# Two transformer blocks in one kernel: weight low parts move from GpSimd to VectorE, and a fold of squares to TensorE

## The chip, the cores and the metric

The kernel runs on one core of a Trainium2 chip. A core has five engines that run side by side, each with its own queue of instructions in program order: TensorE (PE in the profile, with its weight loads as PEld), VectorE (DVE), ScalarE (ACT), GpSimd (POOL) and SyncE (SP), which here only issues transfers. They wait for each other by semaphores. The metric is the device time of one execution in microseconds (us); lower is better.

## What is computed

The reference runs two transformer blocks over 256 tokens (the first with 16 extra ones in front) and 1024 features, all in float32:

```python
# block 1
xn = rms_norm(h, gain0)
proj = xn @ w_in                       # q, k, v of two attentions, forget gate, two gates
o_a, o_b = forgetting_attention(...), stick_breaking_attention(...)
mixed = (sigmoid(g_a) * (o_a @ w_o_fox) + sigmoid(g_b) * (o_b @ w_o_sb)) @ w_out
h = h + rms_norm(mixed, gain1)
u = causal_depthwise_conv(rms_norm(h, gain2) @ w_up, conv_w, conv_b)   # 2 x 2816 features
h = h + rms_norm((gelu(u_gate) * u_val) @ w_down, gain3)
# block 2
proj = rms_norm(h, g_mix) @ w_in_2     # differential attention, retention, two gates
...
return rms_norm(x, g_final)
```

Block 2 goes on with attention, retention, a squared-ReLU feed-forward, a gated embedding and the last norm.

## The kernel before

**Split products.** Every large product is made of three products of a reduced float32 form (`float32r`): each operand is split into a high part (ScalarE's copy into `float32r`) and a low part (the operand less its high part). `mm3`, `feat_tile` and `token_tile` issue high x high (L320, or L333 with tokens as rows), weight low x feature high (L321, L334) and weight high x feature low (L323, L336).

**Weights.** `Weights` streams the weights as slabs of 256 or 512 columns. Each slab is two units (half slabs of 512 KB, one tile of 128 x 1024). SyncE loads a unit into one of `RAW` = 5 raw buffers; `split_unit` has ScalarE make its high part (`whi`, L87); `finish` makes the low parts still owed (`wlo`, L96) and issues the next loads. VectorE makes them, but GpSimd does where `finish` is called with `True`, and each fourth one while `ws.share` is 4. At most two slabs are split ahead. `start` splits one unit (two where the lead is short), and `next` hands a slab to TensorE.

**Order of the work.** The program order is written out by hand. After each tile of products (one bank of PSUM, four banks in turn) `period` runs: it starts a unit, advances the evacuations of earlier tiles by one stage (`side.evac`), lets one side task go on (`side.tick`) and finishes the low part. So on VectorE each tile's evacuation and the unit's low part come one after the other. `linear` runs a list of tiles; with `wave=3` it begins with three tiles chunk by chunk of the 1024 features, so that chunks can be used as they are made.

**The places that the change touches**, in order of time:

- `ev_mix` (L829) evacuates the second attention's output projection: product with the gate, sum, ScalarE's high part of the mixed features, and in its second stage their low part (`xl`, L835), on GpSimd for the first six of eight chunks.
- The next projection (`w_out`) collects sums of squares: VectorE adds the squares up (L400, `acc`), and TensorE sums them over the features with a matrix of ones (L392). After its last tile `period` is called without finishing, and `residual` (L876) follows: statistics (`rstd_narrow`), `ws.finish(True)` (L882), the broadcast of the result (L415), and then `make(k)`, which produces chunk k of the next input: VectorE's product with the gain, the addition to the residual `R` (GpSimd from the second chunk on, L897), ScalarE's high part and square, VectorE's low part. The up projection's first wave of three tiles consumes the chunks as they come.
- The up projection with a causal convolution (22 slabs, 44 tiles; `ev_conv`, L961): per tile VectorE scales the bank (`ur`, L302) and adds two shifted products (`cv`, L308, a pair of instructions), ScalarE adds bias and third tap (L969), and, by kind of tile, ScalarE's gelu or VectorE's product of both halves with its split follows. `ws.share = 4` holds here (L983).
- The down projection (L1012 on) walks four column groups, each over slabs of 6, 8 and 8 feature chunks, for two token tiles. Before it ScalarE loads another function table (L1011). Ahead of the last slab stands `ws.start(2)`, `ws.finish(True)`. Then `down_rstd` and `down_scale` give the normed rows, which TensorE turns (`turn_raw`, L1044).
- Block 2's first products (L1080 on): for token tile t and chunk k, `normed` updates the residual, `high` and `low` split it, and TensorE uses the chunk at once in two banks. For the statistics `squares` has ScalarE square four chunks at a time; after the second four GpSimd folds eight blocks into two (L1065), and `mix_sums` sums these two over the features (L1070); `mix_rstd` makes the reciprocal root from it. For t = 1 two units are started (k = 2 and 4) and finished on GpSimd (k = 3 and 5).

Of the kernel before, what the change touches and what calls it, by code (L numbers as in the profile page):

```python
# [20 lines left out]
KD = D // P  # L21
# [28 lines left out]
class Weights:  # L50
    """Streams weight slabs: DMA, then an exact split into two float32r parts."""

    def __init__(self, nc, raw, hi, lo, plan):
        self.nc, self.rawp, self.hip, self.lop = nc, raw, hi, lo
        self.plan = plan
        self.raw, self.parts = {}, {}
        self.loaded = 0
        self.units = 0
        self.todo = []
        self.at = 0  # L60
        self.share = self.lows = 0

# [27 lines left out]

    def finish(self, idle=False):
        for lo, w, hi in self.todo:
            self.lows += 1
            idle = idle or self.share and self.lows % self.share == 0
            eng = self.nc.gpsimd if idle else self.nc.vector
            eng.tensor_tensor(lo, w, f32(hi), ALU.subtract)  # L96
        self.todo = []
        self.load(self.units + RAW)
# [22 lines left out]
class Side:  # L121
    """Advances evacuations and queued side tasks by one stage per call."""

# [46 lines left out]
def two_blocks_kernel(  # L170
# [64 lines left out]

# [1 line left out]
    tab = cp.tile([P, 256], F32, name="tab")  # L237
# [52 lines left out]

# [1 line left out]
    def bank(pool, tag):  # L292
# [81 lines left out]
    class Sums:  # L374
        """Sums of squares over features, with tokens on the partitions."""

# [47 lines left out]

    def period(gen=None, finish=True):
        ws.start()
        side.evac()
        if gen is not None:
            side.evacs.append((0, gen))
        side.tick()  # L430
        if finish:
            ws.finish()
# [70 lines left out]

# [1 line left out]
    R = cp.tile([P, KD, NQ], F32, name="R")  # L505
# [101 lines left out]

# [1 line left out]
    u4 = unit("u4", shape=(P, KD, L1))  # L609
# [209 lines left out]

# [1 line left out]
    def ev_fox(ps, j):  # L821
# [7 lines left out]
    def ev_mix(ps, j):  # L829
        t = tp_tile("t", NQ)  # L830
        mul(t, ps[:, :NQ], gb[:, j, :])
        add(t, t, ga[:, j, :])
        A.activation(xh[:, j, 0:NQ], t, AF.Copy)
        yield
        (G if j < 6 else V).tensor_tensor(xl[:, j, 0:NQ], t, f32(xh[:, j, 0:NQ]), ALU.subtract)  # L835

# [39 lines left out]
    def residual(sums, after, toks, off, n, gout, gnext, fill):  # L876
        """The next linear's input from a normed residual: a maker of one chunk at a time."""
        side.evac()
        fill(0)
        side.flush()  # L880
        y = sums.rstd()
        ws.finish(True)  # L882
        fill(1)
        pb = at()
        bcast(pb, y, toks)
        fill(2)
        hi = unit("xh", F32R, (P, KD, L1))
        lo = unit("xl", F32R, (P, KD, L1))
        sqs = {}

        def res(k):
            return R[:, k, off:off + n]

        def normed(k, eng):
            t = tp_tile("t", n)
            stt(t, raw[:, k, 0:n], g1(gout + k), pb[:, :n])
            eng.tensor_tensor(res(k), res(k), t, ALU.add)  # L897

        def high(k):
            A.activation(hi[:, k, 0:n], res(k), AF.Identity, scale=g1(gnext + k))  # L900
            sqs[k] = after.tile(n)
            A.activation(sqs[k], res(k), AF.Square)

        def make(k):
            if k == 0:
                normed(0, V)
                normed(1, G)
                high(0)
            if k + 2 < KD:
                normed(k + 2, G)  # L910
            if k + 1 < KD:
                high(k + 1)
            stt(lo[:, k, 0:n], res(k), g1(gnext + k), f32(hi[:, k, 0:n]), ALU.mult, ALU.subtract)
            if k in (4, 6):
                ws.start(1)
            if k in (5, 7):
                ws.finish()
            if k in (0, 1, 5, 6):
                fill(3)
            return sqs[k]  # L920
        return chunks(hi, lo), make
# [11 lines left out]
    def ple_filler(W, stages):  # L933
        """Spreads the embedding's products over a residual's waits: one bank at a time."""
        held = []

        def fill(stage):
            if stage == 3:
                dst, src = held.pop(0)
                A.activation(dst, src, AF.Copy)  # L940
                return
            for t, c in stages[stage]:
                ps = at() if len(held) < 3 else mm()
                ts, cs = slice(t * P, (t + 1) * P), slice(c, c + 512)
                for k in range(2):
                    mm3(ps, ph[:, k, ts], pl[:, k, ts], W[0][:, k, cs], W[1][:, k, cs], k == 0, k == 1)
                held.append((ple[:, t, cs], ps))
        return fill

    box = {}  # L950

# [1 line left out]
    s1 = Sums(TOKQ, acc=True, mixed=True)  # L953
# [7 lines left out]
    def ev_conv(ps, j):  # L961
# [11 lines left out]
        if not val:  # L973
# [8 lines left out]

    ws.share = 4  # L983
    linear(feat_tiles(KF1, X2, 0, NQ), KD, ev_conv, wave=3, make=make, sums=s1,
           after=next_rstd(s1, NQ, [(rb2, 1.0)], box))
    ws.share = 0
    rawt = unit("u7", shape=(P, 2, D))
# [24 lines left out]
    for c in range(4):  # L1012
        pss = [mm(), mm()]
        for k0, nk in DOWN:
            W = ws.next()
            last = k0 + nk == KF1
            if c == 3 and last:
                ws.start(2)
                ws.finish(True)
            for t in range(2):  # L1020
# [9 lines left out]

# [1 line left out]
    hi = unit("xh", F32R, (P, KD, L1))  # L1032
# [27 lines left out]
    def squares(t, i):  # L1060
        A.activation(sqs[:, t, 4 * i:4 * i + 4, :],
                     R[:, 4 * i:4 * i + 4, 2 + t * P:2 + (t + 1) * P], AF.Square)
        if i:
            for n in (4, 2):
                G.tensor_tensor(sqs[:, t, 0:n, :], sqs[:, t, 0:n, :], sqs[:, t, n:2 * n, :], ALU.add)  # L1065

    def mix_sums(t):
        ps = turned[t] = at()
        for i in range(2):
            T.matmul(ps[:, 0:1], sqs[:, t, i, :], ones[:, 0:1], start=i == 0, stop=i == 1)  # L1070

# [12 lines left out]
    for t in range(2):  # L1084
# [3 lines left out]
        for k in range(KD):  # L1088
# [7 lines left out]
            if t == 0:  # L1096
                if k == 1:
                    y = down_rstd(1)
                if k == 2:
                    down_scale(1, y)  # L1100
            elif k in (2, 4):
                ws.start(1)
            elif k in (3, 5):
                ws.finish(True)
            for part in range(2):
# [216 lines left out]

# [1 line left out]
    def ev_brd(ps, j):  # L1324
# [44 lines left out]

# [1 line left out]
    gh = [unit(f"u{i}", F32R) for i in (0, 1, 2, 4)]  # L1371
# [37 lines left out]

# [1 line left out]
    gfin = unit("u0", shape=(P, D))  # L1411
# [90 lines left out]
```

## Time and profile before

| | us |
|---|---|
| median of 3 runs (range) | 951.78 (950.01 to 952.24) |
| profiled execution, first to last instruction (its span; the page gives no other time for it) | 950.2 |
| TensorE busy | 923.9 (97%) |
| VectorE busy | 648.3 (68%) |
| ScalarE busy | 523.5 (55%) |
| GpSimd busy | 91.5 (10%), 75 instructions |
| TensorE clock granted, mean | 0.988 |

The span is the time between the first and last instruction of one profiled execution; the runs are timed from outside and are 1.6 us longer in the median. A busy engine is one with an instruction under way; the products of TensorE are pipelined, so that their durations overlap (0.28 us long, 0.12 us apart). Averages over the whole span mix stages with different limits.

### The profile page before, as it was taken

Reading aid. Unit: us, or ns where it says so; the run is one execution under the profiler, and the core shown is the slowest. Engines: PE = TensorE matmul, PEld = TensorE weight load, DVE = VectorE, ACT = ScalarE, POOL = GpSimd, SP = SyncE. Lnnn points to the kernel's source line nnn. Section 1 sums busy time; section 2 is a strip of 40 time slices with the busy share of each in tenths; the row PEclk is TensorE's granted clock in tenths of the full one; section 3 lists DMA queues with packets and bytes.
Section 4 is the critical chain, followed back from the end, with each engine's and each line's share of the span. In section 5 each row is a group of like instructions: output and inputs, shape, how many; then the busy total and the mean of one; then the engine's idle time right before and its main releaser. Section 6 shows DMA issues by size and latency. Waiting matters only on the chain.

```text
span 950.2 us, 18312 instructions
## 1 busy us (share of the span) xinstructions
PE 923.9 (97%) x7457; PEld 894.6 (94%) x7457; DVE 648.3 (68%) x1150; ACT 523.5 (55%) x948; POOL 91.5 (10%) x75
## 2 busy tenths in 40 slices
PE   7999999999999999899899999999999999999996
PEld 5999988999899999899899999999999999999996
DVE  4667664577699999734767774577787666655546
ACT  5534565466576666545656665445555565544435
POOL 4022100022332222001300000000000000000000
PEclk7999999999999999899999999999999999999998
DMA  8554434456255565565265556455475566565531
GB/s 263 156 156 122 121 90 111 133 180 210 89 156 178 178 179 178 167 208 179 90 202 157 152 170 192 139 165 170 136 225 173 177 200 185 177 209 179 187 130 45
DMA packets 149715, 154.73 MB, mean 163 GB/s; under 512 B 5260, under 2 KB 145808, under 8 KB 149632
## 3 DMA queue, kind: packets, MB, share of 16 engines
q1 hardware_dynamic: 147904, 149.56, 52.4%
q0 software_dynamic: 1376, 3.36, 1.1%
q8 instruction: 58, 0.95, 0.4%
q10 hardware_dynamic: 352, 0.66, 0.2%
q14 instruction: 25, 0.20, 0.1%
HBM read 152.50 MB, written 1.05 MB: 162 GB/s over the span
## 4 chain that ended last, share of the span: by engine, by line
PE 79%; DVE 15%; issue 2%; ACT 2%; DMA 1%; POOL 0%; SPq 0%; DVEq 0%; ACTq 0%
PE mm L320 20%; PE mm L323 19%; PE mm L321 19%; DVE cv L308 5%; DVE wlo L96 4%; PE mm L336 4%; PE mm L334 4%; PE mm L333 4%; DVE ur L302 2%; PE at L671 1%; DVE cv L302 1%; DMA raw<-in_w_in_dram 1%; PE at L735 1%; PE at L1156 1%; DVE u L981 1%
## 5 line engine op out<-in xcount | busy, mean ns | idle before, releaser
L87 ACT ACTIVATE whi<-raw 128x1024 fp32r<-128x1024 f32 (+1 forms) x284 | 292.3, 1047 | 186.5 <-PE mm L323 90.9
L96 DVE TENSOR_TENSOR wlo<-raw,whi 128x1024 fp32r<-128x1024 f32 (+1 forms) x267 | 325.0, 1225 | 100.1 <-ACT whi L87 99.8
L323 PE MATMUL mm<-xl,whi 128*128 128x258 f32 (+2 forms) x1256 | 351.4, 283 | 1.3 <-DVE xl L308 1.3
L320 PE MATMUL mm<-xh,whi 128*128 128x258 f32 (+3 forms) x1192 | 342.8, 288 | 3.4 <-ACT xh L542 3.4
L321 PE MATMUL mm<-xh,wlo 128*128 128x258 f32 (+3 forms) x1192 | 337.5, 284 | 0.3 <-DVE wlo L96 0.3
L323 PEld LDWEIGHTS mm<-xl,whi 128*128 128x128 f32 x1256 | 235.8, 189 | 2.0 <-DVE xl L308 1.7
L320 PEld LDWEIGHTS mm<-xh,whi 128*128 128x128 f32 (+1 forms) x1192 | 225.1, 189 | 7.0 <-ACT xh L542 3.4
L321 PEld LDWEIGHTS mm<-xh,wlo 128*128 128x128 f32 (+1 forms) x1192 | 225.2, 189 | 1.6 <-DVE wlo L96 1.2
L320 PE MATMUL mm<-u,whi 128*128 128x256 f32 (+1 forms) x704 | 198.4, 282 | 0.0
L321 PE MATMUL mm<-u,wlo 128*128 128x256 f32 (+1 forms) x704 | 197.1, 280 | 0.0
L323 PE MATMUL mm<-u,whi 128*128 128x256 f32 (+1 forms) x576 | 162.6, 282 | 0.0
L321 PEld LDWEIGHTS mm<-u,wlo 128*128 128x128 f32 x704 | 133.1, 189 | 0.0
L320 PEld LDWEIGHTS mm<-u,whi 128*128 128x128 f32 x704 | 132.5, 188 | 0.0
L323 PEld LDWEIGHTS mm<-u,whi 128*128 128x128 f32 x576 | 108.4, 188 | 0.0
L333 PE MATMUL mm<-whi,u 128*128 128x256 f32 x240 | 68.7, 286 | 2.4 <-ACT whi L87 2.4
L334 PE MATMUL mm<-wlo,u 128*128 128x256 f32 x240 | 68.9, 287 | 1.5 <-DVE wlo L96 0.9
L336 PE MATMUL mm<-whi,u 128*128 128x256 f32 x240 | 68.6, 286 | 0.0
L308 DVE SCALAR_TENSOR_TENSOR cv<-ur,gc,cv 128x256 f32<-128x256 f32 x88 | 66.3, 756 | 1.6
L96 POOL TENSOR_TENSOR wlo<-raw,whi 128x1024 fp32r<-128x1024 f32 x17 | 40.8, 2405 | 176.1 <-ACT whi L87 94.2
L302 DVE TENSOR_TENSOR u<-mm,rb 128x256 f32<-128x256 f32 (+2 forms) x68 | 28.9, 425 | 40.1 <-PE mm L323 40.1
L333 PEld LDWEIGHTS mm<-whi,u 128*128 128x128 f32 x240 | 46.4, 193 | 2.6 <-ACT whi L87 2.6
L334 PEld LDWEIGHTS mm<-wlo,u 128*128 128x128 f32 x240 | 46.6, 194 | 1.9 <-DVE wlo L96 1.1
(343 smaller groups left out, 1088.4 us busy)
## 6 DMA issues: line engine op xcount, KB each, us to landing
raw<-in_w_in_dram SPq DMA_DIRECT2D x102, 512.0 KB, 3.8
raw<-in_w_ff_dram SPq DMA_DIRECT2D x64, 512.0 KB, 3.9
raw<-in_w_up_dram SPq DMA_DIRECT2D x44, 512.0 KB, 3.6
raw<-in_w_out_dram SPq DMA_DIRECT2D x16, 512.0 KB, 4.4
raw<-in_w_down_dram SPq DMA_DIRECT2D x16, 512.0 KB, 4.8
raw<-in_w_branch_diff_dram SPq DMA_DIRECT2D x8, 512.0 KB, 3.5
raw<-in_w_branch_ret_dram SPq DMA_DIRECT2D x8, 512.0 KB, 3.4
raw<-in_w_ple_gate_dram SPq DMA_DIRECT2D x8, 512.0 KB, 3.8
```

The source lines that it names most:

```text
L87: self.nc.scalar.activation(hi[:, a:b], w, AF.Copy)
L96: eng.tensor_tensor(lo, w, f32(hi), ALU.subtract)
L302: V.tensor_tensor(o, a, b, ALU.mult)
L308: V.scalar_tensor_tensor(out=o, in0=a, scalar=s, in1=b, op0=op0, op1=op1)
L320: T.matmul(ps, sh, mh, start=first, stop=False)
L321: T.matmul(ps, sl, mh, start=False, stop=False)
L323: T.matmul(ps, sh, ml, start=False, stop=last)
L333: T.matmul(ps[:, 0:256], hi, W[0][:, k, :], start=first, stop=False)
L334: T.matmul(ps[:, 0:256], hi, W[1][:, k, :], start=False, stop=False)
L336: T.matmul(ps[:, 0:256], lo, W[0][:, k, :], start=False, stop=last)
L671: T.matmul(S[:, 0:258], k[:, 0:128], q, start=False, stop=False, skip_group_check=True)
L735: T.matmul(o, l, i, start=False, stop=True, skip_group_check=True)
```

## The change

Low parts of weights are always VectorE's: `finish` has no choice of engine any more, and `share` is gone. All eight low parts of the mixed features are VectorE's. In the last tile before the residual no unit is started; one is started behind the statistics and finished after chunk 1. Between the blocks the two units are started at chunks 2 and 5 and finished at 4 and 7. GpSimd folds no squares; TensorE sums all eight blocks. GpSimd keeps its additions to the residual and half of the sums `acc` there.

```diff
-    def finish(self, idle=False):
+    def finish(self):
         for lo, w, hi in self.todo:
-            self.lows += 1
-            idle = idle or self.share and self.lows % self.share == 0
-            eng = self.nc.gpsimd if idle else self.nc.vector
-            eng.tensor_tensor(lo, w, f32(hi), ALU.subtract)
+            self.nc.vector.tensor_tensor(lo, w, f32(hi), ALU.subtract)
...
-    def period(gen=None, finish=True):
-        ws.start()
+    def period(gen=None, split=True):
+        if split:
+            ws.start()
         side.evac()
...
-        if finish:
+        if split:
             ws.finish()
...
-        (G if j < 6 else V).tensor_tensor(xl[:, j, 0:NQ], t, f32(xh[:, j, 0:NQ]), ALU.subtract)
+        V.tensor_tensor(xl[:, j, 0:NQ], t, f32(xh[:, j, 0:NQ]), ALU.subtract)
...
         y = sums.rstd()
-        ws.finish(True)
+        ws.start(1)
         fill(1)
...
-            if k in (5, 7):
+            if k in (1, 5, 7):
                 ws.finish()
...
-    ws.share = 4
     linear(feat_tiles(KF1, X2, 0, NQ), KD, ev_conv, wave=3, make=make, sums=s1,
            after=next_rstd(s1, NQ, [(rb2, 1.0)], box))
-    ws.share = 0
...
                 ws.start(2)
-                ws.finish(True)
+                ws.finish()
...
-        if i:
-            for n in (4, 2):
-                G.tensor_tensor(sqs[:, t, 0:n, :], sqs[:, t, 0:n, :], sqs[:, t, n:2 * n, :], ALU.add)
...
-        for i in range(2):
-            T.matmul(ps[:, 0:1], sqs[:, t, i, :], ones[:, 0:1], start=i == 0, stop=i == 1)
+        for i in range(KD):
+            T.matmul(ps[:, 0:1], sqs[:, t, i, :], ones[:, 0:1], start=i == 0, stop=i == KD - 1)
...
-            elif k in (2, 4):
+            elif k in (2, 5):
                 ws.start(1)
-            elif k in (3, 5):
-                ws.finish(True)
+            elif k in (4, 7):
+                ws.finish()
```

## Rows read from the trace of the kernel before

**Rows 1.** The page, the chain that ended last: share of the span by engine

```profile
PE 79%; DVE 15%; issue 2%; ACT 2%; DMA 1%; POOL 0%; SPq 0%; DVEq 0%; ACTq 0%
```

**Rows 2.** Stretches: length, busy us (instructions) of PE, PEld, DVE, ACT, POOL; clock; DMA

```profile
203.00:216.00 13.00, 13.00 (x110) 12.93 (x109) 11.82 (x22) 6.51 (x12) 7.90 (x8) 1.00 0.55 172
...
311.08:322.85 11.77, 11.77 (x100) 11.77 (x99) 11.63 (x20) 7.69 (x12) 2.40 (x2) 1.00 0.61 181
346.36:358.13 11.77, 11.76 (x98) 11.55 (x97) 11.63 (x20) 7.70 (x12) 2.40 (x2) 1.00 0.61 180
376.00:400.00 24.00, 20.12 (x142) 19.46 (x141) 18.48 (x29) 14.00 (x22) 2.37 (x1) 0.86 0.55 172
392.00:394.00 2.00, 2.00 (x11) 2.00 (x11) 2.00 (x3) 1.62 (x2) 0.00 (x0) 0.50 0.58 176
```

**Rows 3.** Timeline of VectorE: start us, us, engine, line, operation, out<-in, count

```profile
214.80 0.41 DVE L835 TENSOR_TENSOR xl<-t,xh 128x258 fp32r<-128x258 f32 x1
...
233.85 3.42 DVE L96 TENSOR_TENSOR wlo<-raw,whi 128x1024 fp32r<-128x1024 f32 x1
...
309.80 1.22 DVE L96 TENSOR_TENSOR wlo<-raw,whi 128x1024 fp32r<-128x1024 f32 x1
...
311.27 3.01 DVE L308 SCALAR_TENSOR_TENSOR cv<-ur,gc,cv 128x256 f32<-128x256 f32 x2
...
314.87 1.00 DVE L308 SCALAR_TENSOR_TENSOR cv<-ur,gc,cv 128x256 f32<-128x256 f32 x2
...
384.52 0.42 DVE L302 TENSOR_TENSOR ur<-mm,rb 128x258 f32<-128x258 f32 x1
...
445.69 1.59 DVE L308 SCALAR_TENSOR_TENSOR nt<-ny,nh 128x1 f32<-128x1 f32 x1 [0.41 <-ACT ny L362]
...
458.93 1.76 DVE L308 SCALAR_TENSOR_TENSOR nt<-ny,nh 128x1 f32<-128x1 f32 x1
460.73 2.27 DVE L308 SCALAR_TENSOR_TENSOR nr<-nt,ny 128x1 f32<-128x1 f32 x1
```

**Rows 4.** Timeline of GpSimd: in brackets the idle time before and what ended it

```profile
233.76 2.42 POOL L96 TENSOR_TENSOR wlo<-raw,whi 128x1024 fp32r<-128x1024 f32 x1 [17.58 <-ACT whi L87]
...
263.90 4.95 POOL L96 TENSOR_TENSOR wlo<-raw,whi 128x1024 fp32r<-128x1024 f32 x2 [7.69 <-ACT whi L87]
...
311.08 2.40 POOL L96 TENSOR_TENSOR wlo<-raw,whi 128x1024 fp32r<-128x1024 f32 x1 [9.36 <-DVE wlo L96]
...
381.08 2.37 POOL L96 TENSOR_TENSOR wlo<-raw,whi 128x1024 fp32r<-128x1024 f32 x1 [8.83 <-ACT whi L87]
442.52 4.75 POOL L96 TENSOR_TENSOR wlo<-raw,whi 128x1024 fp32r<-128x1024 f32 x2 [59.06 <-ACT whi L87]
...
458.28 4.70 POOL L96 TENSOR_TENSOR wlo<-raw,whi 128x1024 fp32r<-128x1024 f32 x2 [1.06 <-ACT whi L87]
```

**Rows 5.** Timeline of TensorE: in brackets its wait and what ended it

```profile
238.29 0.59 PE L392 MATMUL at<-ones,acc 128*86 128x1 f32 x6 [1.60 <-DVE acc L400]
...
376.83 0.28 PE L333 MATMUL mm<-whi,u 128*128 128x256 f32 x1
...
383.51 0.38 PE L334 MATMUL mm<-wlo,u 128*128 128x256 f32 x1 [0.62 <-POOL wlo L96]
...
390.31 0.39 PE L333 MATMUL mm<-whi,u 128*128 128x256 f32 x1 [2.39 <-ACT whi L87]
...
448.01 1.06 PE L1044 MATMUL at<-tab,u 128*128 128x128 f32 x8 [1.04 <-DVE u L1008]
...
457.83 0.50 PE L1070 MATMUL at<-ones,u 128*128 128x1 f32 x4
458.19 0.36 PE L333 MATMUL mm<-whi,xh 128*128 128x256 f32 x1
...
463.75 0.51 PE L336 MATMUL mm<-whi,xl 128*128 128x256 f32 x2 [2.71 <-DVE xl L308]
```

**Rows 6.** Timeline of ScalarE: the table load before the down projection

```profile
387.91 1.28 ACT L1011 ACT_TABLE_LOAD   x1
```

More of the change, by code (lines that the diff above doesn't have):

```diff
@@ L60, in __init__ @@
         self.at = 0
-        self.share = self.lows = 0
     def load(self, upto):
```

## The prediction

> **What bounds the kernel now.** I read the page's chain first, then the table of stretches, then each engine's own timeline around the seventeen places where GpSimd makes a low part. The chain that ends last is 79% TensorE and 15% VectorE [rows 1]: TensorE sets the pace, and the question is where VectorE makes it wait. In the table of stretches [rows 2] the reader is to see three things. First, TensorE's own rate: 110 products are listed in the 13.00 us from 203, two of them straddling an edge, so 13.00/108 = 0.120 us each. Second, in the feed-forward's up projection VectorE is busy 11.63 us of 11.77, that is, always. One turn of that loop is two slabs: four tiles of 24 products, 96 in all. At 311.08 TensorE still gets 98 products into 11.77 us (100 listed less two straddlers), its free rate; at 346.36 it gets 96, VectorE's rate. So TensorE is barely the faster (96 x 0.120 = 11.52 us against 11.77) and runs on its four banks of slack until they are used up. Third, the bill comes at the end: from 376 to 400 only 142 products are listed in 24.00 us, and at 392 the granted clock is 0.50, the 1.2 GHz level.
>
> The timelines say why VectorE is slow. In each turn it runs one pair of `cv` instructions in 3.01 us where the next pair of the same shape takes 1.00 [rows 3]; the slow pair, at 311.27, starts just behind GpSimd's low part (311.08 for 2.40 us) and gets going when that ends [rows 4]. It is so for all twelve low parts of this projection, from 263.90 to 381.08. The same shows outside it. GpSimd's low part at 233.76 lies over a VectorE low part of 3.42 us where 1.22 is usual. The two at 442.52 lie over a step of 1.59 us on one column. The two at 458.28 lie over two such steps of 1.76 and 2.27 us [rows 3, 4]. TensorE waits behind these: 1.60 us before L392, 1.04 before L1044, 2.71 before L336 [rows 5].
>
> **The up projection, twelve low parts.** On VectorE one costs 1.22 us [rows 3]; the duration overstates it a little, since neighbours overlap at their ends. What goes is the stretch, 3.01 - 1.00 = 2.01 us. VectorE's turn becomes 11.77 - 2.01 + 1.22 = 10.98 us, below TensorE's 11.52: VectorE stops being the bound and catches up. In all it is relieved of 12 x 0.79 = 9.5 us. It now starts the last tile's evacuation at 384.52 [rows 3], 7.7 us after TensorE went on to the down projection at 376.83 [rows 5]; so the lateness goes, and the last tiles wait for TensorE instead.
>
> What hangs on that lateness: ScalarE's table load at 387.91 [rows 6] stands behind the last `cv` work, 3.4 us after that evacuation, and the third down slab's high and low parts behind the load; TensorE ran out of work there and waited 2.39 us, after 0.62 for a GpSimd low part at 383.51 [rows 5]. It can run the first two down slabs without the table: 14 chunks x 2 token tiles x 3 = 84 products, 10.1 us. In before the third slab's high part served TensorE at 390.31, 5.8 us after the last evacuation began, and its low part is 1.22 us more. If TensorE enters the projection near 376 it needs them at 386, so the last evacuation must begin by 379; I put it at 376 to 377. The stall goes, with 2 to 3 us to spare, and with it what followed, a stretch at the lower clock. Its worth: 24.00 us less 140 products at 0.120 is 7.2 us; and the three last turns lost two products each, 6 x 0.12 = 0.7. Sum 7.9 us. Bounds: VectorE saves less per low part and a stall of some 3 us is left (5 us gained), or the last turns also run freer (8.5).
>
> The Perfetto Trace Analysis page of the Trainium skill (Optimizing Scalar/DVE Operations) says that with a saturated VectorE moving some work to ScalarE, or even GpSimd, may pay, though it adds that those two share a read port of SBUF. By the first half this change is wrong and would cost the whole 12 x 1.22 = 14.6 us; by the row, where the move slows VectorE by more than it takes away, it gives 9.5 us of VectorE's time back. The SBUF page (Who interferes with whom) has the sharper form, that a VectorE instruction with two SBUF inputs is blocked for the whole of a GpSimd one; 3.01 us over 2.40 agrees with it.
>
> **The mixed features, six low parts (L835).** TensorE does not stop here now; its windows are full. VectorE takes six more instructions of 0.41 us [rows 3]. Five of them come before the product that frees the bank of the third tile of the next projection's first wave, 5 x 0.41 = 2.0 us; VectorE has 13.00 - 11.82 = 1.2 us idle there [rows 2], and the waves leave no bank over. So TensorE is later by something between nothing and 2.0; I take 0.7. GpSimd's two transfers behind these low parts are issued no later, and are needed several us on.
>
> **The first residual.** The high part of one half slab moves behind the statistics, where ScalarE waits, and costs nothing; its low part goes from GpSimd to VectorE after chunk 1. The 3.42 us instruction becomes 1.22, the sum of squares behind it is done before TensorE asks, and the 1.60 us wait goes. Against it stands 1.22 us in the chain that makes the eight chunks, with the next chunk's low part and GpSimd's next addition queued behind it; between nothing (if TensorE's lag covers it) and 1.22 shows up. I take 0.8. Net 0.8 gained. The raw buffer comes free some ten us later, so one slab load starts later; four more are in hand, so I cost that at nothing; without this cover it would be a few us of DMA.
>
> **Between the blocks.** The two low parts at 442 go on an idle VectorE (nothing runs there until the statistics at 445), so the step of 1.59 shrinks and the wait of 1.04 goes. The two at 458 move to other chunks (started at 2 and 5, finished at 4 and 7), behind the reciprocal root instead of over it; 1.76 + 2.27 us of stretched steps go, and with them the wait of 2.71. The folds leave GpSimd, and TensorE sums eight blocks of squares in place of two. It has four instructions for two now, and the next product starts 0.36 us later [rows 5]: 0.09 each, so six sums more are 12 x 0.09 = 1.08 us, twice 2.2 us. Ends: nothing if they fall into waits, 3.0 by the 0.50 us of four instructions. I take 2.2, since after the waits are gone TensorE has work there all the time. Net 1.04 + 2.71 - 2.2 = 1.6 gained.
>
> **Sum.** -7.9 + 0.7 - 0.8 - 1.6 = -9.6 us. The profiled span is 950.2 us, the runs' median 951.78, so 1.6 us lie around it: 940.6 in a profile, 942.2 in the runs.
>
> **Rivals.**
> - *The stretch is not GpSimd's doing* (the pair waits for ScalarE's `cv`, say), so VectorE pays for the twelve low parts and gets nothing back: 14.6 us in the up projection, and 2.2 of sums: 951.8 + 16.8 = 968.6, slower. It decides from the point where less than 1.22 of the 2.01 us comes back. For it: VectorE is full there. Against: every stretched instruction lies over a GpSimd one, and so do the one-column steps, which have no such partner. Chance 0.03. (It is where the first half of the Trainium skill's sentence on a saturated VectorE, above, would lead.)
> - *The stall at the table load stays*, because the load itself and the chain behind it are too long: then 0.7 + 0.6 + 0.8 - 0.7 + 1.6 = 3.0 gained, 948.8, within the noise. Against: the 2 to 3 us to spare. Chance 0.05.
> - *VectorE's queue takes the place of GpSimd's* in the small stages: mix +1.4, residual 0, between the blocks only 1.04 against 2.2: 7.9 - 1.4 - 1.2 = 5.3 gained, 946.5. For it: low parts now stand in front of chunks that TensorE asks for every 0.7 to 1.1 us. Chance 0.12.
> - *The small costs are hidden*: mix 0, residual 1.6 gained, sums free: 13.3 gained, 938.5. Chance 0.10.
>
> **Numbers.** The forecast, 942.2 (its own range 939.5 to 944.5), has 0.70. The range 938 to 947 takes in the bounds of the unknown costs and the two near rivals, and leaves out some 0.15. A measurement of this kernel tells about 0.3%, 2.9 us. The forecast, the third and the fourth case are faster by more (0.92); the second is about that bound (0.05); the first is slower (0.03).
>
> **What the new profile would show.** The pairs of `cv` at 1.00 us throughout; VectorE with idle time in the up projection; 98 products in each 11.77 us of it to the end; the last evacuation within 1 us of TensorE's last tile; no gap and no lower clock after the table load; no wait before L392, and none of over 1 us before L336; L1070 with some 1.1 us more each time. I am wrong if VectorE's instructions are stretched without GpSimd, if the down projection still halts, or if new waits appear behind VectorE's low parts in the residual.

## The result and the profile after

The changed kernel takes 940.25 us (median of 4 runs, 939.66 to 942.12) beside 951.92 us of the kernel before (4 runs, 950.01 to 952.24): ratio 0.9883, 95% interval 0.9872 to 0.9895. It is 1.2% faster. The forecast was 942.2 us with a range of 938 to 947. The profiled execution has a span of 940.3 us (its own time is 942.12, 1.8 more), 9.9 less than before; the forecast for the span was 940.6.

First the page of the changed kernel: the chain that ended last, by engine, and then the busy time of each engine (us, share, instructions).

```profile
PE 94%; DVE 3%; ACT 1%; DMA 1%; issue 0%; POOL 0%; SPq 0%; DVEq 0%; ACTq 0%
...
PE 924.5 (98%) x7481; PEld 895.4 (95%) x7481; DVE 637.3 (68%) x1173; ACT 524.7 (56%) x948; POOL 40.4 (4%) x48
```

VectorE was 15% of the chain [rows 1] and is 3%. Of the 27 instructions that GpSimd gave up (75 became 48) VectorE took 23, the low parts, and yet its busy time fell, from 648.3 us to 637.3: an instruction that is held in the middle of its work counts as busy. The group of `cv` instructions shows it. It is the same 88 instructions of the same shape in both kernels, at 756 ns each before (66.3 us in all) and at 480 ns after:

```profile
L304 DVE SCALAR_TENSOR_TENSOR cv<-ur,gc,cv 128x256 f32<-128x256 f32 x88 | 42.0, 480 | 1.6
```

The 24.3 us that went are 2.02 for each of the twelve low parts that GpSimd made there.

The table of stretches of the changed kernel (columns as in [rows 2]) has the same places:

```profile
203.00:216.00 13.00, 12.41 (x104) 12.22 (x103) 12.73 (x27) 5.52 (x11) 0.00 (x0) 1.00 0.52 166
...
346.00:358.00 12.00, 12.00 (x103) 12.00 (x102) 11.43 (x22) 7.98 (x13) 0.00 (x0) 1.00 0.58 180
...
376.00:400.00 24.00, 24.00 (x205) 24.00 (x204) 14.47 (x20) 13.10 (x20) 0.00 (x0) 1.00 0.62 189
392.00:394.00 2.00, 2.00 (x20) 2.00 (x19) 1.20 (x1) 2.00 (x5) 0.00 (x0) 1.00 0.62 212
```

From 346 to 358, 101 products (103 listed less two straddlers) run in 12.00 us, 0.119 each: TensorE's own rate, and VectorE has idle time. In the first line, where VectorE took over the mixed features' low parts, it goes the other way: 104 products are listed where 110 were, and VectorE is idle for 0.27 us where it was for 1.18. The biggest gain is in the third line: 205 products from 376 to 400 where 142 were, at the full clock where 0.86 was the mean and 0.50 the lowest.

To split the 9.9 us, I marked the same products in both TensorE timelines and compared the stretches between them:

| stretch between marks of TensorE | before, us | after, us | difference |
|---|---|---|---|
| start to the first product of `w_out` | 212.91 | 212.71 | -0.2 |
| to the sums of squares held for the residual | 25.38 | 24.35 | -1.0 |
| to the first product of the up projection | 7.68 | 7.37 | -0.3 |
| up projection, first wave of three tiles | 10.52 | 11.95 | +1.4 |
| rest of the up projection | 120.34 | 119.51 | -0.8 |
| down projection, to the turn behind it | 71.18 | 62.46 | -8.7 |
| turn and first products of block 2, to the second broadcast | 24.40 | 24.31 | -0.1 |
| the rest | | | -0.2 |

The marks themselves, in TensorE's timeline of the changed kernel, with the waits that are left around them:

```profile
214.22 0.35 PE L316 MATMUL mm<-xh,whi 128*128 128x258 f32 x1 [0.59 <-DVE t L298]
...
237.06 0.40 PE L388 MATMUL at<-ones,acc 128*86 128x1 f32 x4
...
249.19 0.63 PE L319 MATMUL mm<-xl,whi 128*128 128x258 f32 x3 [0.34 <-DVE xl L304]
...
252.36 0.63 PE L319 MATMUL mm<-xl,whi 128*128 128x258 f32 x3 [0.73 <-DVE xl L304]
...
254.82 0.39 PE L319 MATMUL mm<-xl,whi 128*128 128x258 f32 x1 [1.12 <-DVE xl L304]
...
375.89 0.28 PE L329 MATMUL mm<-whi,u 128*128 128x256 f32 x1
...
438.35 1.03 PE L1039 MATMUL at<-tab,u 128*128 128x128 f32 x8
...
448.15 1.84 PE L1062 MATMUL at<-ones,u 128*128 128x1 f32 x16
449.85 0.36 PE L329 MATMUL mm<-whi,xh 128*128 128x256 f32 x1
```

The large waits of [rows 5] are gone: no bracket stands at the held sums (1.60 before) or at the turn (1.04), and none at the products of block 2 where 2.71 stood. New are a wait of 0.59 near the start of `w_out` and more waiting in the first wave of the up projection (0.34, 0.73 and 1.12). In the kernel before, that wave had these two:

```profile
252.47 0.62 PE L323 MATMUL mm<-xl,whi 128*128 128x258 f32 x3 [0.18 <-DVE xl L308]
254.94 0.62 PE L323 MATMUL mm<-xl,whi 128*128 128x258 f32 x3 [1.11 <-DVE xl L308]
```

VectorE's timeline of the changed kernel gives the reasons:

```profile
245.01 1.66 DVE L92 TENSOR_TENSOR wlo<-raw,whi 128x1024 fp32r<-128x1024 f32 x1
...
309.38 0.99 DVE L304 SCALAR_TENSOR_TENSOR cv<-ur,gc,cv 128x256 f32<-128x256 f32 x2
...
376.13 0.42 DVE L298 TENSOR_TENSOR ur<-mm,rb 128x258 f32<-128x258 f32 x1
...
437.23 0.22 DVE L304 SCALAR_TENSOR_TENSOR nt<-ny,nh 128x1 f32<-128x1 f32 x1 [0.41 <-ACT ny L358]
...
450.58 0.22 DVE L304 SCALAR_TENSOR_TENSOR nt<-ny,nh 128x1 f32<-128x1 f32 x1
450.83 0.16 DVE L304 SCALAR_TENSOR_TENSOR nr<-nt,ny 128x1 f32<-128x1 f32 x1
```

The pair of `cv` takes 0.99 us each time. The last tile's evacuation starts at 376.13, 0.24 us after the down projection began (7.7 before). The steps on one column, which took 1.59, 1.76 and 2.27 us [rows 3], take 0.16 to 0.22. But the low part that moved into the residual takes 1.66 us, not 1.22: GpSimd still adds to the residual there, and its timeline shows an instruction group right under it:

```profile
243.26 2.33 POOL L894 TENSOR_TENSOR R<-R,t 128x258 f32<-128x258 f32 x3 [26.31 <-DVE t L304]
```

### The profile page after: what moved, and what is told of

It reads as the page before. It is cut to its first block, busy times and chain, and to the rows that moved or that the text cites. A ratio compares the mean times of both kernels' runs of the same rounds, so it can differ in the third digit from the quotient of the medians.

```text
span 940.3 us, 18333 instructions
## 1 busy us (share of the span) xinstructions
PE 924.5 (98%) x7481; PEld 895.4 (95%) x7481; DVE 637.3 (68%) x1173; ACT 524.7 (56%) x948; POOL 40.4 (4%) x48
## 4 chain that ended last, share of the span: by engine, by line
PE 94%; DVE 3%; ACT 1%; DMA 1%; issue 0%; POOL 0%; SPq 0%; DVEq 0%; ACTq 0%
PE mm L316 24%; PE mm L319 23%; PE mm L317 23%; PE mm L332 5%; PE mm L329 5%; PE mm L330 5%; PE at L668 1%; DVE wlo L92 1%; PE at L732 1%; PE at L1148 1%; DMA raw<-in_w_in_dram 1%; PE at L740 0%; PE at L666 0%; PE at L669 0%; DVE xl L304 0%
## 5 line engine op out<-in xcount | busy, mean ns | idle before, releaser
L92 DVE TENSOR_TENSOR wlo<-raw,whi 128x1024 fp32r<-128x1024 f32 (+1 forms) x284 | 343.2, 1217 | 100.2 <-ACT whi L86 99.9
L332 PE MATMUL mm<-whi,u 128*128 128x256 f32 x240 | 67.4, 281 | 0.0
L329 PE MATMUL mm<-whi,u 128*128 128x256 f32 x240 | 67.4, 281 | 0.0
L332 PEld LDWEIGHTS mm<-whi,u 128*128 128x128 f32 x240 | 45.1, 188 | 0.0
L329 PEld LDWEIGHTS mm<-whi,u 128*128 128x128 f32 x240 | 45.1, 188 | 0.0
L304 DVE SCALAR_TENSOR_TENSOR cv<-ur,gc,cv 128x256 f32<-128x256 f32 x88 | 42.0, 480 | 1.6
```

Source lines behind the costliest of these rows:

```text
L92: self.nc.vector.tensor_tensor(lo, w, f32(hi), ALU.subtract)
L304: V.scalar_tensor_tensor(out=o, in0=a, scalar=s, in1=b, op0=op0, op1=op1)
L329: T.matmul(ps[:, 0:256], hi, W[0][:, k, :], start=first, stop=False)
L332: T.matmul(ps[:, 0:256], lo, W[0][:, k, :], start=False, stop=last)
```

## The experiments

Theory A is that of the prediction: VectorE's instructions with two inputs are held while GpSimd reads, so each GpSimd low part costs VectorE more than VectorE would need to make it; the gain is the stall behind the up projection. Theory B: VectorE has too little time in any case, and the gain comes from somewhere else, such as the moved starts, the folds or the short steps. Four kernels part these.

**One line of the change alone.** The kernel before, with VectorE making all low parts in the up projection and nothing else changed:

```diff
-    ws.share = 4
+    ws.share = 0
```

> The kernel before with one edit: in the up projection no low part goes to GpSimd. Theory (GpSimd's low part blocks VectorE's two-input instructions): every pair of cv takes 1.00 us, VectorE is on time at the end, the stall and the lower clock after the table load go: 8 to 9 us faster than before, about 943.5. Rival 1 (the slow pair is not GpSimd's doing): twelve low parts more on a full VectorE, 14 us slower, 966. Rival 2 (the table load itself makes the stall): about 1 us faster, 951.

Measured: 943.83 us (943.34 to 945.49), ratio 0.9919, interval 0.9903 to 0.9936. The rows, the `cv` group and the stretch behind the up projection:

```profile
L308 DVE SCALAR_TENSOR_TENSOR cv<-ur,gc,cv 128x256 f32<-128x256 f32 x88 | 42.0, 480 | 1.6
...
376.00:400.00 24.00, 24.00 (x205) 24.00 (x204) 15.08 (x20) 13.10 (x20) 0.00 (x0) 1.00 0.64 195
```

This one line brings 7.2 us, by medians, of the whole gain, takes the stretch out of `cv`, and fills the 24 us behind the up projection with the same 205 products as the full change.

**All of the change but that line.** The changed kernel, with each fourth low part of the up projection on GpSimd again (eleven, one fewer than in the kernel before):

```diff
-            self.nc.vector.tensor_tensor(lo, w, f32(hi), ALU.subtract)
+            self.lows += 1
+            eng = self.nc.gpsimd if self.share and self.lows % self.share == 0 else self.nc.vector
+            eng.tensor_tensor(lo, w, f32(hi), ALU.subtract)
...
+    ws.share = 4
     linear(feat_tiles(KF1, X2, 0, NQ), KD, ev_conv, wave=3, make=make, sums=s1,
            after=next_rstd(s1, NQ, [(rb2, 1.0)], box))
+    ws.share = 0
```

> The changed kernel with one part undone: in the up projection each fourth low part is GpSimd's again. Theory: the slow pairs, the late VectorE, the stall and the lower clock are back, some 8 us slower than the changed kernel: 948.5, or 3 us faster than before. If the small stages carried the gain instead: 941 to 943.

Measured: 948.23 us (945.05 to 949.31), ratio 0.9960, interval 0.9944 to 0.9977. The stretched `cv` group is back, and in TensorE's timeline so are both waits behind the up projection:

```profile
L307 DVE SCALAR_TENSOR_TENSOR cv<-ur,gc,cv 128x256 f32<-128x256 f32 x88 | 64.4, 734 | 1.6
...
382.09 0.39 PE L333 MATMUL mm<-wlo,u 128*128 128x256 f32 x1 [0.64 <-POOL wlo L95]
...
388.88 0.57 PE L332 MATMUL mm<-whi,u 128*128 128x256 f32 x1 [2.38 <-ACT whi L87]
```

So is the lower clock behind them, in this kernel's table of stretches:

```profile
392.00:394.00 2.00, 2.00 (x12) 2.00 (x11) 2.00 (x3) 0.66 (x2) 0.00 (x0) 0.50 0.77 241
```

The two halves, 0.9919 and 0.9960, multiply to 0.9879, inside the interval of the whole change (0.9872 to 0.9895): nothing clear of the noise is left to be explained by their working together. The larger half is the one that theory A names, so theory B falls as the main cause; what is true of it is the smaller half, 2.8 us by medians.

**GpSimd reading, with nothing asked of it.** The changed kernel, with an extra subtraction on GpSimd beside each fourth low part of the up projection, eleven in all. VectorE makes all low parts, as in the changed kernel; the result of the extra work goes to `scr`, a part of a buffer that is no longer in use, and no part of the computation is left out.

```diff
             self.nc.vector.tensor_tensor(lo, w, f32(hi), ALU.subtract)
+            self.lows += 1
+            if self.share and self.lows % self.share == 0:
+                n = min(1024, hi.shape[1])
+                self.nc.gpsimd.tensor_tensor(self.scr[:, :n], f32(hi[:, :n]), f32(hi[:, :n]), ALU.subtract)
...
+        if j == 0:
+            ws.share, ws.scr = 4, raw.rearrange("p k n -> p (k n)")[:, 0:1024]
...
+    ws.share = 0
```

> The changed kernel, and beside every fourth low part of the up projection GpSimd also runs one subtraction of 128x1024 whose result nobody reads (its inputs are a high part, in SBUF). VectorE's own work is unchanged and nothing waits for GpSimd. Theory (GpSimd's reads block VectorE): one pair of cv in each turn takes 3 us again, the turn is 10.98 + 2.01 = 13.0 us, above TensorE's 11.5: about 10 x 1.4 us and the stall at the end, 14 to 21 us slower than the changed kernel, 954 to 961. Rival (before was slow because its low parts came late from GpSimd, or for the split of work): no change, 940.

Measured: 954.55 us (951.34 to 958.03), ratio 1.0028, interval 1.0012 to 1.0045: 14.3 us more than the changed kernel by medians, and slower than the kernel before. The `cv` group, one GpSimd subtraction, the pair of VectorE instructions over it, and a stretch:

```profile
L309 DVE SCALAR_TENSOR_TENSOR cv<-ur,gc,cv 128x256 f32<-128x256 f32 x88 | 58.9, 673 | 1.6
...
311.85 1.90 POOL L97 TENSOR_TENSOR u<-whi 128x1024 f32<-128x1024 f32 x1 [10.54 <-ACT whi L87]
...
312.02 2.52 DVE L309 SCALAR_TENSOR_TENSOR cv<-ur,gc,cv 128x256 f32<-128x256 f32 x2
...
300.00:312.00 12.00, 11.38 (x95) 11.17 (x94) 11.86 (x20) 7.57 (x12) 1.46 (x2) 1.00 0.60 176
```

The `cv` pair starts at 312.02 and ends at 314.54, 0.79 after the subtraction does (313.75), little less than the 0.99 that a free pair takes; VectorE is full again, and TensorE gets 93 products (95 listed less two straddlers) into 12.00 us where it had 101. Beside the changed kernel's marks, the up projection is 7.4 us longer and the down projection up to the turn 6.1. In the kernel before, too, the slow pair ended 0.80 us behind the low part it lay over (311.27 for 3.01 us over 311.08 for 2.40) [rows 3, 4].

**GpSimd writing only.** The same places, but three memsets on GpSimd, released by a one-column copy on ScalarE; again nobody uses what they write.

```diff
+                self.nc.scalar.activation(self.scr[:, 0:1], f32(hi[:, 0:1]), AF.Copy)
+                for _ in range(3):
+                    self.nc.gpsimd.memset(self.scr, 0.0)
...
+        if j == 0:
+            ws.share, ws.scr = 4, raw.rearrange("p k n -> p (k n)")[:, 0:1024]
...
+    ws.share = 0
```

> As the run in which GpSimd reads, but GpSimd only writes: three memsets of 128x1024, some 2.8 us together, at the same places, released by a one-column copy on ScalarE. If only GpSimd's reads block VectorE: pairs of cv at 1.00 us, within 1 us of the changed kernel, 940 to 941. If any GpSimd work blocks it: like the run in which GpSimd reads, 954 or more.

Measured: 940.83 us (939.99 to 941.90), ratio 0.9890, interval 0.9875 to 0.9905, the changed kernel's time. GpSimd is busy longer each time than with the subtraction, and VectorE's instructions under it keep their lengths:

```profile
307.90 2.98 POOL L98 MEMSET u<- 128x1024 f32 x3 [7.94 <-ACT u L96]
...
309.03 1.00 DVE L310 SCALAR_TENSOR_TENSOR cv<-ur,gc,cv 128x256 f32<-128x256 f32 x2
309.94 1.22 DVE L93 TENSOR_TENSOR wlo<-raw,whi 128x1024 fp32r<-128x1024 f32 x1
```

So it is not GpSimd's being busy that holds VectorE, nor its writes. What the subtraction has beside these is two inputs that it reads. That the reading counts and not the subtracting is argued: no GpSimd instruction that computes without reading, or reads without computing, was run.

**How much lateness the down projection bears.** The forecast saw 2 to 3 us to spare. The changed kernel, with idle VectorE additions of 128 x 1024 ahead of the evacuation of the 42nd of 44 tiles, two in one kernel (shown) and six in the other, `range(6)` (their result is not used):

```diff
+        if j == 41:
+            scr = raw.rearrange("p k n -> p (k n)")[:, 0:1024]
+            for _ in range(2):
+                V.tensor_tensor(scr, scr, scr, ALU.add)
```

> The changed kernel with two further VectorE instructions (128x1024, 1.14 us each, result unused) ahead of the evacuation of the third last tile of the up projection: VectorE is 2.3 us late there. The low part behind the table load has 2.9 us to spare, so no stall: within 0.5 us of the changed kernel, 940.5. If any lateness at the end is paid for: 942.5.

> The same with six such instructions: VectorE is 6.8 us late, about as late as before the change (7.7). Theory (the lateness alone makes the stall): 3 to 4 us of stall, and up to 2.5 us more if the clock falls to its lower level: 943.5 to 947. Rival (GpSimd's low parts or the table load make it, not the lateness): 940 to 941.

Measured: 940.52 us with two (939.88 to 944.48; ratio 0.9886, interval 0.9862 to 0.9911), no loss; the last evacuation starts 1.98 us after the down projection's first product, where it was 0.24. With six 946.28 us (944.52 to 948.92; 0.9941, 0.9918 to 0.9963). There the last evacuation starts at 385.42, 7.25 us after the down projection's first product (378.17), nearly as late as in the kernel before, and the waits of [rows 5] come back:

```profile
385.56 0.39 PE L330 MATMUL mm<-wlo,u 128*128 128x256 f32 x1 [1.04 <-DVE wlo L92]
...
391.21 0.38 PE L329 MATMUL mm<-whi,u 128*128 128x256 f32 x1 [1.24 <-ACT whi L86]
...
392.47 0.39 PE L330 MATMUL mm<-wlo,u 128*128 128x256 f32 x1 [0.88 <-DVE wlo L92]
```

The stretch behind the up projection, in the same trace:

```profile
376.00:400.00 24.00, 20.70 (x168) 19.89 (x167) 19.73 (x30) 13.56 (x22) 0.00 (x0) 1.00 0.39 118
```

This makes a stall out of VectorE's lateness alone, with no GpSimd near. From its first product to the turn the down projection takes 66.82 us, 4.4 more than in the changed kernel and 4.4 less than in the kernel before. The clock stayed at 1.00 through these waits of 3.2 us, so this kernel does not show the lower clock that stood behind the stall in the kernel before; that part of the 7.2 us was not reproduced by lateness alone. By medians the six additions cost 6.0 us, more than these 4.4. The profiled execution, the slowest of the four, had the clock at 0.50 from 256 to 260 as well, in the residual, long before the additions; what the other three lost beside the stall was not seen.

**The two terms that came out too small.** The first wave cost +1.4 us where 0.8 was forecast, and the sums between the blocks gave back nearly all of the waits that went. First, the low part of the residual's unit made at once, behind the statistics, instead of after chunk 1:

```diff
         ws.start(1)
+        ws.finish()
...
-            if k in (1, 5, 7):
+            if k in (5, 7):
```

> The changed kernel, but in the residual the low part is made at once behind the statistics instead of after chunk 1. VectorE is idle there for 1.05 us (it waits for the broadcast), and the first wave now ends 1.4 us later against its start than before the change. Theory (the low part in the chunks' chain costs that 1.4 us, partly because GpSimd's addition blocks it): about 1.1 us faster than the changed kernel, 939.1. Rival (the chain is slow whatever stands in it): no change, 940.3.

Measured: 939.93 us (938.44 to 941.07), ratio 0.9866, interval 0.9848 to 0.9885. The times don't part it from the changed kernel, but the trace does: the first wave takes 10.84 us in place of 11.95, and the low part runs at its free length, before GpSimd's first addition:

```profile
240.88 1.23 DVE L92 TENSOR_TENSOR wlo<-raw,whi 128x1024 fp32r<-128x1024 f32 x1 [0.24 <-ACT whi L86]
```

Second, the changed kernel with GpSimd's fold of squares back, and so two sums in place of eight:

```diff
+        if i:
+            for n in (4, 2):
+                G.tensor_tensor(sqs[:, t, 0:n, :], sqs[:, t, 0:n, :], sqs[:, t, n:2 * n, :], ALU.add)
...
-        for i in range(KD):
-            T.matmul(ps[:, 0:1], sqs[:, t, i, :], ones[:, 0:1], start=i == 0, stop=i == KD - 1)
+        for i in range(2):
+            T.matmul(ps[:, 0:1], sqs[:, t, i, :], ones[:, 0:1], start=i == 0, stop=i == 1)
```

> The changed kernel, but GpSimd folds the squares again and TensorE sums two blocks. Theory (the six further sums cost TensorE 1.34 us each time, and the folds block VectorE only where TensorE has other work): 2.0 to 2.7 us faster than the changed kernel, 938. Rival (the folds block VectorE where TensorE waits): as much lost as gained, 940.

Measured: 938.69 us (938.31 to 940.49), ratio 0.9862, interval 0.9846 to 0.9879: 1.6 us better by medians, less than was expected. From the first sums to the second broadcast 12.68 us pass, where the changed kernel needs 14.51. The sums are short again, and the fold is late by 0.54 us only the second time:

```profile
446.08 0.50 PE L1065 MATMUL at<-ones,u 128*128 128x1 f32 x4
...
455.36 0.61 PE L1065 MATMUL at<-ones,u 128*128 128x1 f32 x4 [0.54 <-POOL u L1060]
```

**Both, and two more steps.** The last four kernels are the two edits together; these with six `xl` low parts of the mixed features on GpSimd again; the changed kernel once more, run beside these two; and, run later, the two edits with all sums `acc` on VectorE, so that GpSimd stretches VectorE less in the first wave.

```diff
-        V.tensor_tensor(xl[:, j, 0:NQ], t, f32(xh[:, j, 0:NQ]), ALU.subtract)
+        (G if j < 6 else V).tensor_tensor(xl[:, j, 0:NQ], t, f32(xh[:, j, 0:NQ]), ALU.subtract)
...
-    s1 = Sums(TOKQ, acc=True, mixed=True)
+    s1 = Sums(TOKQ, acc=True)
```

> The changed kernel with both improvements that the single runs pointed to: the low part at once behind the statistics, and the squares folded by GpSimd again. In the traces the single runs gave 1.1 and 1.8 us; if they add, 2.9 us faster than the changed kernel run beside it (about 937.3). If one hides the other: 938.5.

> The same, and the first six low parts of the mixed features are GpSimd's again. Theory (moving them to VectorE holds up a bank and costs TensorE 0.6 to 0.7 us): 0.6 us faster than the run with both (936.7). Rival (they block VectorE as much as they relieve it): no change to it.

> The changed kernel itself, unedited, as the mark for the two runs beside it on the same chip: 940.3, with a scatter of about 1 us.

> The run with both improvements, and the three sums of squares that GpSimd makes in the residual go to VectorE as well. They read two tiles in SBUF and lie over VectorE's work there: a wait of 0.64 us and stretches of 0.45 to 0.53 us on four instructions, about 2.5 us against 3 x 0.34 us that VectorE takes over. Theory: the first wave of the up projection ends 0.5 to 1.2 us sooner against its start, 936.5. Rival (VectorE is the longer chain there either way): no change, 937.3, or 1 us slower.

| kernel | median us (range) | ratio to before (95% interval) |
|---|---|---|
| both edits | 937.27 (936.26 to 943.12) | 0.9855 (0.9835 to 0.9874) |
| both, mixed features on GpSimd | 938.16 (937.56 to 939.34) | 0.9859 (0.9845 to 0.9872) |
| the changed kernel again | 939.59 (939.29 to 942.73) | 0.9880 (0.9865 to 0.9895) |
| both, sums on VectorE (run later) | 937.89 (937.60 to 938.12) | 0.9862 (0.9845 to 0.9878) |

Both edits together have the lowest median, 2.3 us below the changed kernel run beside them (2.9 was expected), though the intervals still overlap. The other two steps missed their expectations. With the mixed features on GpSimd, the stretch from `w_out` to the held sums is 0.74 us shorter than with both edits alone (23.63 against 24.37), as expected, but it was given back in the residual: TensorE comes earlier, and there GpSimd's sum stands behind VectorE's low part and TensorE waits 0.72 us for it. Moving the sums `acc` to VectorE changed nothing measurable in the time, and the first wave, at 11.43 us, is longer than the 10.84 of the kernel with the early low part alone. The residual's second low part, made after chunk 5, stayed stretched (1.66 us, as at 252.23 in the changed kernel), so GpSimd's additions to `R` are enough to stretch it. One row from GpSimd's timeline of the first kernel, one from VectorE's of the second:

```profile
251.78 1.64 POOL L396 TENSOR_TENSOR acc<-acc,sq 128x258 f32<-128x258 f32 x1 [1.10 <-DVE xl L304]
```

```profile
249.28 1.66 DVE L92 TENSOR_TENSOR wlo<-raw,whi 128x1024 fp32r<-128x1024 f32 x1
```

## Why the prediction was right, point by point

**The cause** was right. A GpSimd low part takes 2.0 us from VectorE, where VectorE makes it in 1.22. One line that moves the twelve low parts brings 7.2 us; GpSimd subtractions that serve nothing cost 14.3; GpSimd writes in the same places cost nothing. The rival in which the stretch is not GpSimd's doing is refuted by that pair of kernels. The Trainium skill's sentence in Perfetto Trace Analysis (Optimizing Scalar/DVE Operations), that a saturated VectorE may gain by offloading even to GpSimd, does not hold here: the kernel with the offload alone put back is 8 us slower by medians (948.23 against 940.25). Its warning in the same place, that moving work between VectorE and GpSimd, which share a read port of SBUF, might not help, does. The SBUF page of the Trainium skill (Who interferes with whom) says that VectorE's second SBUF input contends with GpSimd instructions that read SBUF, and not with those that only write; the runs agree, with 673 ns per `cv` against 481.

**Up projection, forecast -7.9.** The trace gives -0.8 for the up projection past its first wave (forecast -0.7) and -8.7 from there to the turn. This second stretch holds two terms of the forecast, the tail (-7.2) and the wait of 1.04 before the turn: -8.2. Together they are right within half a us. The kernel with the one line alone, in which a wait of 0.99 stays before the turn, takes 63.60 us there, 7.6 less than before: that is the tail by itself. The rates came out as forecast too: 101 products in 12.00 us, 0.119 each, and the last evacuation 0.24 us after TensorE's last tile. The stall at the table load, a rival at 0.05, is gone: ScalarE loads the table at 379.52 and starts the third slab's high part right behind it.

```profile
379.52 1.28 ACT L1006 ACT_TABLE_LOAD   x1
380.81 3.48 ACT L86 ACTIVATE whi<-raw 128x1024 fp32r<-128x1024 f32 x4
```

The time to spare was worked out as 2 to 3 us past a last evacuation at 376 to 377; two idle additions, 1.98 us of lateness, cost nothing; six, 7.25 us of lateness, cost about 6 us by medians. The runs bracket the edge and don't say where it is.

**Mixed features, forecast +0.7.** The stretch to the held sums fell by 1.0 us while the wait of 1.60 in it went, so +0.6; TensorE's new wait of 0.59 for the bank stands where the forecast put it, at the third tile of the next projection's first wave. The 0.7 was picked between nothing and 2.0, so that it came this close is luck.

**First residual, forecast -0.8 net, measured -0.5.** The wait of 1.60 us went, and the up projection starts 0.3 us sooner behind the sums. The term that was mis-sized is the chain's cost: 0.8, "between nothing and 1.22", was 1.4 in the first wave. The bound used the free length of the low part. But the part moved under GpSimd's additions to the residual, which the change leaves there, and took 1.66 us: the mechanism that the prediction had just described for seventeen other places. The kernel that makes the low part before those additions gets 1.1 us back in the trace. Here one of the forecast's own signs of being wrong came true in part: new waits behind VectorE in the residual, of 0.34 and 0.73 us.

**Between the blocks, forecast -1.04 before the turn and -0.5 behind it, the latter measured -0.1.** Both waits went. The sums were mis-sized: sixteen instructions take 1.70 us to the next product (448.15 to 449.85) where four took 0.36, so 1.34 more each time and not 1.08; each costs 0.106 us, not 0.09. Twice 1.34 is the 2.7 us that the wait of 2.71 had cost. So the moved starts bring the gain here and the moved fold gives it back: the kernel that puts the fold back and keeps the moved starts is 1.8 us better in the trace. The third rival, VectorE's queue in place of GpSimd's in the small stages, was true in part (the first wave), but too small to move the forecast.

**The sum** of the terms was -9.6 us, and the spans differ by 9.9. Residual and sums gave 0.7 to 0.8 less than forecast, the tail 0.5 more, and the rest is tenths, two of them before the first edit. That the misses nearly cancel is luck. By medians the gain is 11.7 us; the profiled execution of the changed kernel, at 942.12, is the slowest of its four runs, 1.9 above their median, which covers the difference. Where such a difference lies, the changed kernel run once more shows, with a span of 937.4. It reaches the first product of `w_out` 3.0 us sooner than the 212.71 of the table:

```profile
209.69 0.28 PE L316 MATMUL mm<-xh,whi 128*128 128x258 f32 x1
```

From there on both executions take 727.6 to 727.7 us and agree in every stretch of the table to 0.1. So scatter of this size arises ahead of the first edit. Behind that mark the change is worth 9.7 us (737.3 to 727.6); that the other 2 us of the medians are its work is not shown.

## What to carry to other kernels

When two engines read the same memory side by side, cost an offload by what it does to the instructions under it, not by the work that it takes away: compare the duration of one shape with and without the neighbour. And when a piece of work is moved, take its length at the new place, with the neighbours it gets there, not at the old one. A late engine that TensorE outruns for 100 us sends its bill at the next point where the slack is used up, here a table load and the split behind it, so look for a stall's cause far ahead of it.

## What the runs showed of the hardware that was not expected

- Steps on a single column are held as well as large ones: 0.16 to 0.22 us free, 1.59, 1.76 and 2.27 under GpSimd's low parts [rows 3, 4]. The first ends at 447.28, where GpSimd's pair of low parts ends at 447.27, and the last at 463.00, where GpSimd's ends at 462.98. The step just ahead of the second, which reads one tile (from PSUM), was not held, though it lies under the same low part (VectorE, kernel before):

```profile
458.67 0.16 DVE L360 TENSOR_SCALAR nh<-at 128x1 f32<-128x1 f32 x1 [0.26 <-ACT ny L359]
```

- The hold works in both directions: GpSimd's sum of 128 x 258 took 1.64 us over VectorE's 128 x 1024 low part in the kernel with the mixed features on GpSimd, and 0.86 in the kernel with the early low part alone.
- GpSimd's memsets, 2.98 us for three, did not stretch VectorE at all (1.00 us for a pair).
- The granted clock fell in the lightly loaded residual in some executions and not in others. In the profile of the kernel with both edits it was 0.50, the 1.2 GHz level, at 254 and 258, and that execution took 943.12 us where the median is 937.27; its mean clock was 0.988, that of the three fastest executions of the kernel 0.993 to 0.997. The stretch ahead of the fall has TensorE half idle (0.98 us of 2.00):

```profile
252.00:254.00 2.00, 0.98 (x5) 0.98 (x6) 2.00 (x5) 1.29 (x2) 1.23 (x2) 0.80 0.30 65
254.00:256.00 2.00, 2.00 (x13) 2.00 (x12) 1.38 (x1) 0.00 (x0) 0.30 (x1) 0.50 0.56 198
...
258.00:260.00 2.00, 2.00 (x11) 2.00 (x11) 0.64 (x4) 0.00 (x0) 0.00 (x0) 0.50 0.19 66
```

In the changed kernel run once more TensorE was idle as much there (busy for 0.88 us of 2.00 from 250 to 252), and the clock stayed at 1.00. What decides between the two courses is open.
